# First MLP of a two-layer backbone: another order of the weight sums and of the squares, and other places for some pieces of the conditioning

## The chip, the cores and the metric

The kernel runs on one core of a Trainium2 chip. The metric is the time on the device, in microseconds, of one execution: the median of several runs. The engines are named as in the profile: PE multiplies matrices (PEld is its loading of weights), DVE, ACT and POOL do the elementwise work, SP issues most of the DMA transfers.

## What is computed

Two layers of width 1024 run over 512 latent and 256 context tokens, 768 rows in all. Each layer has a mixer (pooling in the first, attention in the second) and an MLP with 4096 hidden columns and a squared ReLU. Shift, scale and gate of every sub-layer come from a conditioning vector through the matrix `w_ada`. The reference, cut to what the change touches:

```python
def ada_mods(cond, w, b):
    m = (jax.nn.silu(cond) @ w + b)[..., None, :]
    return jnp.split(m, N_MOD, axis=-1)          # SH1 SC1 GT1 SH2 SC2 GT2

def modulate(h, shift, scale):
    return h * (1.0 + scale) + shift

def sq_relu_mlp(h, w_in, w_out):
    return jnp.square(jax.nn.relu(h @ w_in)) @ w_out
```

## The kernel before

**Precision.** Every operand of a large product is split into a high and a low part. One product of two operands is three matmuls: high by high, high by low, low by high. A split is a copy on ACT (the high part, `CAST` in the trace) and a subtraction on DVE (the low part).

**Phase one of the first MLP** (`mlp0`, the loop over g from 2 to 15) makes 256 hidden columns in each step, a *group*, for 768 tokens. It uses a seven-product scheme for 2 by 2 blocks, so each group is seven *chains* of 12 matmuls (`Seven.chain`), numbered 0 to 6 here, each 128x384. The weight operands of a group are the blocks B11, B21, B22 and the sums T1 = B12 − B11, T2 = B22 − T1, T3 = B22 − B12, T4 = B21 − T2, all split. `weights_sums(g + 1, raw)` makes those of the next group while the seven chains of this one run: the B pair and the pair T1, T2 go into `units`, and T3, T4 and B22 into `ra` (odd groups) or `rb` (even groups). Chain 1 uses T1, chain 2 T2, chain 3 B21, chain 4 T3, chain 5 B22 and chain 6 T4.

`Seven.run` issues the chains, copies each bank where the next chain needs it, and calls `behind(n)` between them. The lists in `behind` hold the steps of `weights_sums`, the sums over rows of a finished pair of groups (`left_sums`, four in each even group, written to DRAM by POOL's queue for phase two), and the conditioning dots. The two hidden rows `r0` and `r1` of a group go through a ReLU and a square on ACT into one of two `hiddens` tiles. `r0`, `r1` and the two tiles of differences come from a pool of three work tiles, in the order T1/T2, r1, T3/T4, r0.

**Phase two** (`Halves.run`) multiplies the hidden rows by the second matrix: 49 multiplies of 18 matmuls 128x512. In step j it starts the transfer for j + 5 (`load`), multiplies j, and prepares the operands for j + 3 (`prepare`: two copies on ACT, two or three subtractions on DVE). Multiplies 0 to 13 are the first pass, 14 to 27, 28 to 41 and 42 to 48 the others.

**The conditioning of the second layer** is made in *pieces* of 1 MB of `w_ada`, 256 columns each. A piece is loaded (`ask`) and then multiplied on DVE by a row of the conditioning vector and summed (`ada_dot`, a `CUSTOM_DVE` instruction over 128x1024 with a short read of the sum behind it): two such dots for a piece that only the latents need, four for one that the context needs too. 24 pieces go this way: 14 in phase one (52 dots), 10 in phase two (20 dots). The last gate, GT2 of layer 1, is instead summed in the output stage of attention by `ada_sum` (per piece eight multiply-adds 128x256, a transpose and a reduction on DVE) and finished by `ada_fin` with four small matmuls on PE in the second MLP. The gate and the other parts of layer 0 that are needed early use PE (`ada_mm`, `ada_rows`, `ada_sel`, `ada_mods`: matmuls 32x512 or 32x256, a transpose on DVE, four matmuls with `sel`, and a short finish).

**What sets the order.** In phases one and two the order of each engine's instructions is that of the program text (`pin(True)`). Elsewhere a planner places the steps by numbers given to `at` and `st.at`. The raw weights and pieces share a pool of three 1 MB tiles, `rawp`, in the order of their issue on SP's queue.

**The output stage of attention** (`output`) projects the heads (`psy`, bank by bank into `acc` on DVE), adds the result to the residual rows `xr` (L411), norms them (L637, or L635 on ACT) and transposes them on PE (`psx`) for the second MLP.

## Time and profile before

| what | us |
|---|---|
| median of 3 runs | 1181.74 (1181.52 to 1184.62) |
| the profiled execution's own time | 1181.55 |
| span of its trace | 1179.4 |
| phase one, first matmul of g = 2 to the first of phase two | 109.25 to 363.57 |
| phase two, to the first matmul behind it | 363.57 to 575.97 |
| output stage of attention, about | 793 to 843 |

The span is the time between the first and the last instruction that the trace shows; the profiled execution's own time holds 2.15 us more around it. The page of the profile gives the busy time of each engine and groups of instructions; the timeline lists instructions with their start, duration and, in brackets, the idle time before them and what ended it.

### The profile page before, as it was taken

How to read it: one execution, taken by the hardware profiler on the slowest of the kernel's cores; microseconds unless marked ns; L12 is line 12 of the kernel's file. 1: busy time of each engine (PE TensorE's matmuls, PEld its weight loads, DVE VectorE, ACT ScalarE, POOL GpSimd, SP SyncE). 2: the span in 40 equal slices, each digit the busy share in tenths (PEclk: the TensorE clock that was granted, in tenths of full speed). 3: DMA queues.
4: the chain of work that ended last, by engine and by line, in shares of the span. 5: the costliest groups of instructions: out<-in, count | busy, mean ns of one | idle time of the engine just before them, and what ended most of it. 6: DMA issues, size and time to landing. Idle time of an engine off the chain costs nothing.

```text
span 1179.4 us, 15819 instructions
## 1 busy us (share of the span) xinstructions
PE 1119.8 (95%) x6030; PEld 969.1 (82%) x6030; DVE 928.2 (79%) x1319; ACT 618.1 (52%) x1035; POOL 105.3 (9%) x176
## 2 busy tenths in 40 slices
PE   7999788888899999999999999999999999999997
PEld 6779788877888877788888889998988888888886
DVE  5788787788777978997778679968677789778886
ACT  6686354454446444343476357763577346435523
POOL 1230010110110000000032210001100000000001
PEclk9999999999999999999999999999999999999999
DMA  9975554554649999996612101105334233213203
GB/s 376 418 291 133 189 191 168 218 201 174 232 150 347 385 360 352 369 385 237 257 63 81 59 14 59 50 1 196 134 134 143 69 110 143 108 36 143 107 26 117
DMA packets 52506, 213.12 MB, mean 181 GB/s; under 512 B 7408, under 2 KB 10304, under 8 KB 37840
## 3 DMA queue, kind: packets, MB, share of 16 engines
q1 hardware_dynamic: 45824, 185.52, 43.1%
q0 software_dynamic: 6608, 26.61, 6.1%
q8 instruction: 47, 0.77, 0.3%
q14 instruction: 27, 0.22, 0.0%
HBM read 178.16 MB, written 33.96 MB: 180 GB/s over the span
## 4 chain that ended last, share of the span: by engine, by line
PE 72%; DVE 13%; ACT 6%; issue 4%; DMA 2%; POOL 2%; SPq 0%; ACTq 0%; DVEq 0%; POOLq 0%
PE psin L682 14%; PE pso L94 12%; PE pso L1275 11%; PE psin L94 9%; PE pso L950 5%; PE psq L1398 4%; PE psy L1682 3%; PE po L1658 3%; DVE work L94 3%; PE pss L1617 3%; DVE acc L94 2%; DVE waste L94 2%; PE pspt L1639 2%; DVE units L94 2%; DMA raw<-in_w_ada 1%
## 5 line engine op out<-in xcount | busy, mean ns | idle before, releaser
L94 PE MATMUL pso<-ra,sums 128*128 128x512 f32 x594 | 139.0, 394 | 4.1 <-DVE ra L94 2.2
L94 PEld LDWEIGHTS pso<-ra,sums 128*128 128x128 f32 x594 | 112.3, 190 | 29.8 <-DVE ra L94 4.3
L94 DVE CUSTOM_DVE_ANT_0 waste<-raw,crow 128x1024 f32<-128x1024 f32 (+1 forms) x72 | 88.0, 1222 | 11.6 <-DMA raw<-in_w_ada 10.4
L682 PE MATMUL psin<-ra,rb 128*128 128x512 f32 (+1 forms) x310 | 87.8, 360 | 0.0
L1275 PE MATMUL pso<-units,pairs 128*128 128x512 f32 x336 | 82.7, 389 | 0.0
L94 ACT CAST ra<-work 128x1024 fp32r<-128x1024 f32 x34 | 35.6, 1047 | 83.3 <-DVE work L94 81.6
L682 PE MATMUL psin<-ra 128*128 128x512 f32 (+1 forms) x256 | 76.5, 376 | 0.0
L1275 PEld LDWEIGHTS pso<-units,pairs 128*128 128x128 f32 x336 | 63.1, 188 | 13.1
L1279 DVE TENSOR_TENSOR acc<-acc,pso 128x512 f32<-128x512 f32 x72 | 48.7, 682 | 26.3 <-PE pso L1275 26.3
L94 PE MATMUL psin<-sums,units 128*128 128x384 f32 x336 | 63.2, 338 | 4.5 <-ACT psin L94 3.6
L94 PE MATMUL psin<-ra,units 128*128 128x384 f32 x340 | 65.8, 343 | 0.0
L94 PEld LDWEIGHTS psin<-sums,units 128*128 128x128 f32 x336 | 58.2, 188 | 7.6 <-ACT psin L94 6.1
L682 PEld LDWEIGHTS psin<-ra,rb 128*128 128x128 f32 x310 | 55.6, 189 | 8.7
L94 PEld LDWEIGHTS psin<-ra,units 128*128 128x128 f32 x340 | 62.3, 196 | 0.0
L94 ACT ACTIVATE work<-psin 128x384 f32<-128x384 f32 x28 | 13.8, 492 | 91.5 <-PE psin L94 60.5
L94 PE MATMUL pso<-ra,rb 128*128 128x512 f32 x252 | 59.3, 391 | 2.2 <-DVE ra L94 2.2
L242 POOL TENSOR_SCALAR ms<-ss 128x1 f32<-128x1 f32 x15 | 9.7, 645 | 567.7 <-ACT junk L229 547.6
L94 PEld LDWEIGHTS pso<-ra,rb 128*128 128x128 f32 x252 | 47.1, 188 | 13.3 <-DVE ra L94 3.2
L94 DVE TENSOR_TENSOR ra<-work,ra 128x1024 fp32r<-128x1024 f32 x34 | 41.7, 1226 | 19.1 <-ACT ra L94 19.1
L682 PE MATMUL psin<-rb,rb 128*128 128x512 f32 (+1 forms) x155 | 55.9, 362 | 0.6 <-DVE rb L1751 0.6
L682 PEld LDWEIGHTS psin<-ra 128*128 128x128 f32 x256 | 47.1, 188 | 8.7
L1398 PE MATMUL psq<-units,ra 128*128 128x512 f32 x216 | 52.4, 393 | 0.0
(328 smaller groups left out, 2688.3 us busy)
## 6 DMA issues: line engine op xcount, KB each, us to landing
raw<-in_w_ada SPq DMA_DIRECT2D x48, 1024.0 KB, 9.6
raw<-in_w_mlp_in SPq DMA_DIRECT2D x32, 1024.0 KB, 5.1
lefts<-acc POOLq DMA_DIRECT2D x48, 384.0 KB, 5.8
raw<-in_w_mlp_out SPq DMA_DIRECT2D x18, 1024.0 KB, 5.7
wide<-lefts SPq DMA_DIRECT2D x38, 384.0 KB, 6.9
wide<-in_w_mlp_out SPq DMA_DIRECT2D x21, 512.0 KB, 6.3
halfway<-work POOLq DMA_DIRECT2D x14, 512.0 KB, 7.3
raw<-in_w_mlp_out SPq DMA_DIRECT2D x14, 512.0 KB, 7.6
```

The lines of the kernel that those rows point to most:

```text
L94: return lambda *args, **kw: self.tc.keep_in_program_order(f(*args, **kw))
L242: gp.tensor_scalar(out=ms[:, 0:1], in0=ss[:, parts - 1:parts], scalar1=rest, scalar2=EPS, op0=ALU.add, op1=ALU.add)
L682: te.matmul(ps[:, bank, o:o + ln], w[:, k, fs], rhs, start=start, stop=(k == KT - 1 and n == 2), skip_group_check=len(ks) < KT or self.paired)
L950: te.matmul(pss[h][:, 0:cols[h][1]], a[:, f, ts_], w[:, f, cols[h][0]:sum(cols[h])], start=(n == 0 and not seeded[t]), stop=(n == len(seq) ...
L1275: te.matmul(ps, a, w, start=(m == 0), stop=(m == len(seq) - 1))
L1279: ve.tensor_tensor(out=M[n][:, t], in0=M[n][:, t], in1=ps, op=ALU.add)
L1398: te.matmul(ps, a[:, k, sl], w[:, k % 4, :], start=(k == 0 and n == 0), stop=(k == KT - 1 and n == 2))
L1617: te.matmul(ps[:, c2, 0:384], a[:, sl], b[:, kv, 384 * c2:384 * c2 + 384], start=(n == 0), stop=(n == 2))
L1639: te.transpose(ps[:, j, :], p[:, k * P:(k + 1) * P], ident)
L1658: te.matmul(po[:, 0:256], v, p, start=(n == 0), stop=(n == len(seq) - 1))
L1682: te.matmul(ps, a[:, k, sl], w[:, k % 4, o:o + width], start=(k == 0 and n == 0), stop=(k == KT - 1 and n == 2))
```

## The change

In words, by place:

- *Phase one, weights.* One subtraction 128x1024 makes T1 and T3 together; then the B pair is split, then T1/T3 (now in `units`), and later T2 and T4 are made (two subtractions 128x512) and split with B22 into `ra` or `rb`. There are three subtractions for the sums in place of four.
- *Phase one, rows.* `r0` is written by its ReLU straight into the hidden rows and squared there, so that a group uses three work tiles. The ReLU of `r1` and both squares of a group are issued in the next group, behind its chain 0. Three of the row sums stand behind chain 2 and the fourth behind chain 4. The dots stand at the end of a group, behind chains 5 and 6.
- *Pieces.* Phase one has 12 pieces (40 dots), in the order two of four dots, one of two; they go to groups 2 to 13. Phase two has 5 (10 dots), asked at j = 5, 11, 16, 21 and 25. Seven pieces (SH2 1 to 3 and the four of GT2 of layer 1) are loaded and multiplied by dots in the output stage, with the conditioning row in `gate`; `ada_sum` and `ada_fin` are gone. GT2 of layer 0 goes through PE in phase two, in two halves: two loads of 1 MB each at j = 2 and 15, eight matmuls three steps later, the transpose a step behind them, `sel` after the next, then the finish.

In the rows that follow, L94 (before) and L95 (after) are the helper that issues phases one and two in program order, and other numbers move by some lines between the two kernels.

**Phase one, ACT, from one odd group's end into the even group behind it** (`work<-work` is the ReLU of `r1`, `acc<-` are squares or, after, the ReLU of `r0`; `units` holds the weight splits). Before:

```order
L94 CAST rb<-raw 128x512
L94 ACTIVATE work<-psin 128x384
L94 ACTIVATE work<-work 128x768
L94 ACTIVATE acc<-work 128x768 x2
L94 COPY psin<-psin 128x384
L94 CAST units<-raw 128x1024
L94 COPY work<-psin 128x384
L94 CAST units<-work 128x1024
L94 COPY psin<-psin 128x384
L94 ACTIVATE work<-psin 128x384
L94 CAST ra<-work 128x2x4x128
L94 COPY work<-psin 128x384
```

The same place of the changed kernel:

```order
L95 CAST rb<-raw 128x512
L95 ACTIVATE acc<-psin 128x384
L95 CAST units<-raw 128x1024
L95 COPY psin<-psin 128x384
L95 CAST units<-work 128x1024
L95 ACTIVATE work<-work 128x768
L95 ACTIVATE acc<-work 128x768
L95 ACTIVATE acc<-acc 128x768
L95 COPY work<-psin 128x384
L95 COPY psin<-psin 128x384
L95 ACTIVATE acc<-psin 128x384
L95 CAST ra<-work 128x2x4x128
```

The two splits into `units` stand ahead of the ReLU of `r1` and of both squares, which stood ahead of them; and the first ReLU (`<-psin`) writes `acc`, the hidden rows, in place of a work tile.

**Phase one, DVE, an even group** (`ISA waste<-` with the short row behind it is a dot; `acc<-acc` are row sums; `work<-raw` and `work<-raw,work` make the T's). Before, from its last dot on:

```order
L94 ISA waste,mods_94<-raw,crow 128x1024
L94 ISA mods_94 128x1
L94 TENSOR_TENSOR work<-raw 128x512
L94 TENSOR_TENSOR work<-raw,work 128x512
L94 TENSOR_TENSOR ra<-work,ra 128x2x4x128
L94 TENSOR_TENSOR acc<-acc 128x768
L94 TENSOR_TENSOR work<-work 128x384
L94 TENSOR_TENSOR ra<-raw,ra 128x4x128
L94 TENSOR_TENSOR acc<-acc 128x768
L94 TENSOR_TENSOR work<-work,psin 128x384
L94 TENSOR_TENSOR acc<-acc 128x768 x2
```

After, from its first subtraction to the first dot:

```order
L95 TENSOR_TENSOR work<-raw 128x1024
L95 TENSOR_TENSOR units<-raw,units 128x1024
L95 TENSOR_TENSOR units<-work,units 128x1024
L95 TENSOR_TENSOR work<-raw,work 128x512 x2
L95 TENSOR_TENSOR acc<-acc 128x768 x3
L95 TENSOR_TENSOR ra<-work,ra 128x2x4x128
L95 TENSOR_TENSOR work<-work 128x384
L95 TENSOR_TENSOR ra<-raw,ra 128x4x128
L95 TENSOR_TENSOR acc<-acc 128x768
L95 TENSOR_TENSOR work<-work,psin 128x384
L95 ISA waste,mods_95<-raw,crow 128x1024
```

The dots have gone from the middle of the group to its end, three of the four row sums stand together ahead of the low part of T2/T4, and T1/T3 is one instruction.

**Phase two, PE** (`pso` are the multiplies, 18 matmuls each; `psada` the gate of layer 0). From the start of the phase in the changed kernel; before, there are no `psada` rows at this place:

```order
L95 MATMUL pso<-sums 128x512 x18
L95 MATMUL pso<-sums,rb 128x512 x18
L95 MATMUL pso<-ra,rb_103 128x512 x36
L95 MATMUL pso<-ra,sums 128x512 x36
L95 MATMUL psada<-raw,cond 32x512 x8
L95 MATMUL pso<-ra,sums 128x512 x36
L95 MATMUL psada<-work,sel 32x2x4 x4
L95 MATMUL pso<-ra,sums 128x512 x18
L95 MATMUL pso<-ra,rb_103 128x512 x36
L95 MATMUL pso<-ra,sums 128x512 x90
L95 MATMUL pso<-ra,rb_103 128x512 x36
L95 MATMUL pso<-ra,sums 128x512 x18
```

Eight matmuls 32x512 stand behind multiply 5, and four with `sel` behind multiply 7; the second half stands the same way behind multiplies 18 and 20. On DVE the transpose that `sel` needs stands behind the two dots of step 6:

```order
L95 TENSOR_TENSOR rb<-acc,rb 128x1536
L95 ISA waste,mods_95<-raw,crow 128x1024
L95 ISA mods_95 128x1
L95 ISA waste,mods_95<-raw,crow 128x1024
L95 ISA mods_95 128x1
L95 STREAM_TRANSPOSE work<-psada 128x512
L95 TENSOR_TENSOR rb_103<-wide,rb_103 128x768
L95 TENSOR_TENSOR ra<-wide,ra 128x1024
```

**Output stage, DVE** (`rb<-raw` are splits of weights, `rows` the work of `ada_sum`). Before, from the first residual to the second:

```order
L411 SCALAR_TENSOR_TENSOR xr<-acc,rs,xr 128x1024
L326 TENSOR_SCALAR rows<-raw,cond 128x256
L408 TENSOR_TENSOR acc<-psy,gate 128x512
L326 TENSOR_SCALAR rows<-raw,cond 128x256
L331 SCALAR_TENSOR_TENSOR rows<-raw,cond,rows 128x256 x4
L637 TENSOR_SCALAR acc<-xr,rs 128x1024
L331 SCALAR_TENSOR_TENSOR rows<-raw,cond,rows 128x256 x4
L1700 TENSOR_TENSOR rb<-raw,rb 128x1024
L331 SCALAR_TENSOR_TENSOR rows<-raw,cond,rows 128x256
L408 TENSOR_TENSOR acc<-psy,gate 128x512
L331 SCALAR_TENSOR_TENSOR rows<-raw,cond,rows 128x256 x5
L411 SCALAR_TENSOR_TENSOR xr<-acc,rs,xr 128x1024
```

The changed kernel, from the first residual to the second:

```order
L385 SCALAR_TENSOR_TENSOR xr<-acc,rs,xr 128x1024
L382 TENSOR_TENSOR acc<-psy,gate 128x512
L324 ISA raw,mods_95<-raw,gate 128x1024
L324 ISA mods_95 128x1
L324 ISA raw,mods_95<-raw,gate 128x1024
L324 ISA mods_95 128x1
L382 TENSOR_TENSOR acc<-psy,gate 128x512
L611 TENSOR_SCALAR acc<-xr,rs 128x1024
L1699 TENSOR_TENSOR rb<-raw,rb 128x1024
L332 TENSOR_TENSOR mods_95<-mods_95,vec 128x8
L385 SCALAR_TENSOR_TENSOR xr<-acc,rs,xr 128x1024
```

Of the seven pairs of dots one stands ahead of the stage's splits, one among them and the rest between the additions of the banks (`acc<-psy`), the last behind the first residual; `ada_sum` is gone.

The diff, cut to its core:

```diff
+LATER, ALONE = 5, 9
...
+    def ada_mm(i, m, j, w=2, zs=None, raws=None):
...
+            raw = (raws[z] if raws else raw_load(w_ada[i, m, j + z])).rearrange("p (k n) -> p k n", n=w * P)
...
-    def ada_sum(i, m, j, nc_, part):
-        raw = raw_load(w_ada[i, m, j]).rearrange("p (k n) -> p k n", n=256)
...
-        for k in range(1, KT):
-            for c, r in enumerate(rows):
-                ve.scalar_tensor_tensor(out=r, in0=raw[:, k, :], scalar=cond[:, k, c:c + 1], in1=r,
-                                        op0=ALU.mult, op1=ALU.add)
...
-        def difference():
-            tt, t1, t2 = low(0)
-            ve.tensor_tensor(out=t1, in0=b12, in1=b11, op=ALU.subtract)
-            ve.tensor_tensor(out=t2, in0=b22, in1=t1, op=ALU.subtract)
-
-        def difference2():
-            tu, t3, t4 = low(1)
-            ve.tensor_tensor(out=t3, in0=b22, in1=b12, op=ALU.subtract)
-            ve.tensor_tensor(out=t4, in0=b21, in1=k4(w[0][:, 512:1024]), op=ALU.subtract)
-
-        steps = [lambda: put(home[:, 0:2048], rv[:, 0], 1024), difference,
-                 lambda: put(home[:, 2048:4096], k4(w[0]), 1024), difference2,
-                 lambda: put3(0, 2, w[1].rearrange("p (m k n) -> p m k n", m=2, n=P)),
-                 lambda: put3(2, 1, b22.unsqueeze(1))]
+        words = lambda z: z.rearrange("p (m k n) -> p m k n", m=2, n=P)
+
+        def first_two():
+            w[0] = work_tile()
+            ve.tensor_tensor(out=words(w[0]), in0=rv[:, 1].rearrange("p (m k) n -> p m k n", m=2),
+                             in1=rv[:, :, 0:4], op=ALU.subtract)
+
+        def last_two():
+            w[1] = work_tile()
+            t2, t4 = (k4(w[1][:, 512 * m:512 * m + 512]) for m in range(2))
+            ve.tensor_tensor(out=t2, in0=b22, in1=k4(w[0][:, 0:512]), op=ALU.subtract)
+            ve.tensor_tensor(out=t4, in0=b21, in1=t2, op=ALU.subtract)
+
+        steps = [first_two, lambda: put(home[:, 0:2048], rv[:, 0], 1024),
+                 lambda: put(home[:, 2048:4096], k4(w[0]), 1024), last_two,
+                 lambda: put3(0, 2, words(w[1])), lambda: put3(2, 1, b22.unsqueeze(1))]
...
-            behind(0)
+            behind(1)
             self.chain(e, 1, True, True)
             r1 = work_tile()[:, 0:TOK]
             sc.copy(r1[:, 0:HN], e)
-            behind(1)
+            behind(2)
             self.chain(a, 2, False, False)
             sc.copy(c, a)
-            behind(2)
+            behind(3)
             self.chain(b, 3, False, True)
-            r0 = work_tile()[:, 0:TOK]
             sc.activation(r0[:, 0:HN], b, AF.Relu)
-            behind(3)
+            behind(4)
             self.chain(a, 4, False, False)
             sc.copy(r1[:, HN:TOK], a)
             ve.tensor_tensor(out=r1[:, HN:TOK], in0=r1[:, HN:TOK], in1=r1[:, 0:HN], op=ALU.add)
-            behind(4)
+            behind(5)
             self.chain(c, 5, False, True)
             ve.tensor_tensor(out=r1[:, 0:HN], in0=r1[:, 0:HN], in1=c, op=ALU.add)
-            behind(5)
+            behind(6)
             self.chain(a, 6, False, True)
             sc.activation(r0[:, HN:TOK], a, AF.Relu)
-            sc.activation(r1, r1, AF.Relu)
-            for f, r in enumerate((r0, r1)):
-                sc.activation(self.to[:, f, :], r, AF.Square)
-            behind(6)
+            behind(7)
+
+            def squares():
+                sc.activation(r1, r1, AF.Relu)
+                sc.activation(to1, r1, AF.Square)
+                sc.activation(r0, r0, AF.Square)
+
+            return squares
...
-            behind = [[] for _ in range(7)]
+            behind = [[] for _ in range(8)]
             if g < NG - 1:
                 steps, products = weights_sums(g + 1, raw)
                 for n, z in enumerate(steps):
-                    behind[(0, 0, 1, 2, 3, 4)[n]].append(z)
+                    behind[(0, 0, 1, 2, 4, 5)[n]].append(z)
+
+            def rows_done(squares=squares, g=g):
+                squares()
+                if g % 2 and g < 2 * PAIRS:
+                    left_keep(g // 2, 0, hiddens[0][:, :, 0:HN])
+                if g % 2 == 0 and 2 < g <= 2 * PAIRS:
+                    due[:] = left_sums(g // 2 - 1, *hiddens)
+
+            behind[1].append(rows_done)
             if g % 2 == 0:
-                for n, z in enumerate(due):
-                    behind[(3, 4, 5, 5)[n]].append(z)
+                behind[3].append(lambda: [due[n]() for n in range(3)])
+                behind[5].append(lambda: due[3]())
             if asked:
                 for n, z in enumerate(asked.pop(0)):
-                    behind[(1, 6)[n]].append(z)
+                    behind[6 + n].append(z)
             if g < NG - 2:
                 raw = raw_load(w_mlp_in[0, g + 2])
-            if g < NG - 1:
+            if g < NG - 1 and len(work) > LATER:
                 ask(*work.pop(0))
-            else:
+            if g == NG - 1:
                 chain.begin()
-                behind[4].append(lambda: chain.prepare(0))
-                behind[6].append(lambda: chain.prepare(1))
-            seven.run(lambda z: [f() for f in behind[z]])
-            if g < 2 * PAIRS:
-                if g % 2:
-                    due = left_sums(g // 2, *hiddens)
-                else:
-                    left_keep(g // 2, 0, hiddens[0][:, :, 0:HN])
+                behind[5].append(lambda: chain.prepare(0))
+                behind[7].append(lambda: chain.prepare(1))
+            squares = seven.run(lambda z: [f() for f in behind[z]])
             if g == 4:
                 head_gains()
             if g == 8:
                 ve.tensor_scalar(out=grow[:, 0, :], in0=grow[:, 0, :], scalar1=float(HD) ** -0.5, scalar2=None, op0=ALU.mult)
+        squares()
         chain.run()
...
-                if work and j % 2 and j > 2:
+                if work and j in (5, 11, 16, 21, 25):
                     ask(*work.pop(0))
+                for n, k in enumerate((2, 15)):
+                    what = (0, GT2, 2 * n)
+                    if j == k:
+                        wide_raws = [raw_load(w_ada[0, GT2, 2 * n + z]) for z in range(2)]
+                    elif j == k + 3:
+                        ada_mm(*what, 4, None, wide_raws)
+                    elif j == k + 4:
+                        ada_rows(*what)
+                    elif j == k + 5:
+                        ada_sel(*what)
+                    elif j == k + 6:
+                        ada_mods(*what)
...
-            if p == 1:
-                ada_fin(1, GT2, parts[1], 1)
...
-    work = [(i, m, j, 2) for i, m in ((0, GT2), (1, SC1), (1, SH1)) for j in range(4)]
-    work += [(1, m, j, 1) for m in (GT1, SC2, SH2) for j in range(4)]
+    alone = [(1, m, j, 1) for m in (GT1, SC2, SH2) for j in range(4)]
+    duals = [(1, m, j, 2) for m in (SC1, SH1) for j in range(4)]
+    work = [z for n in range(4) for z in (duals[2 * n], duals[2 * n + 1], alone[n])] + alone[4:ALONE]
+    late_work = alone[ALONE:] + [(1, GT2, j, 1) for j in range(4)]
+
+    def ask_late(i, m, j, nc_):
+        raw = raw_load(w_ada[i, m, j])
+        for b in range(2):
+            ada_dot(i, m, j, nc_, raw, [gate[:, 1, :]], raw[:, D * b:D * b + D], b)
...
+        at(38, lambda: sy.dma_start(gate[:, 1, :], silu[0].partition_broadcast(P)))
...
-        parts[1] = small.tile([P, 32], F32, tag="part", name="part", bufs=1)
-        for j in range(4):
-            at((7, 12, 17, 25)[j], ada_sum, 1, GT2, j, 1, parts[1][:, 8 * j:8 * j + 8])
+        for n, what in enumerate(late_work):
+            at((3, 6.5, 10, 13.5, 17, 21, 25)[n], ask_late, *what)
```

## The prediction

> **What bounds the kernel now.** I read the page first (busy time, then the chain that ended last), and then the timeline of single engines in the stages that the change touches.

> ```profile
> PE 1119.8 (95%) x6030; PEld 969.1 (82%) x6030; DVE 928.2 (79%) x1319; ACT 618.1 (52%) x1035; POOL 105.3 (9%) x176
> ...
> PE 72%; DVE 13%; ACT 6%; issue 4%; DMA 2%; POOL 2%; SPq 0%; ACTq 0%; DVEq 0%; POOLq 0%
> ```

> PE is the bound, but 28% of the chain that ended last runs over others. The timeline of PE in phase one says where: one odd group (203.59 to 222.93), the even one behind it, and the last three chains.

> ```profile
> 109.25 2.59 PE L94 MATMUL psin<-ra,units 128*128 128x384 f32 x14
> ...
> 203.59 2.24 PE L94 MATMUL psin<-ra,units 128*128 128x384 f32 x12
> ...
> 208.43 2.36 PE L94 MATMUL psin<-sums,units 128*128 128x384 f32 x12 [0.52 <-ACT psin L94]
> ...
> 213.60 0.45 PE L94 MATMUL psin<-sums,ra 128*128 128x384 f32 x1 [0.72 <-ACT psin L94]
> ...
> 220.01 3.12 PE L94 MATMUL psin<-ra 128*128 128x384 f32 x12 [1.98 <-ACT work L94]
> 222.93 3.10 PE L94 MATMUL psin<-ra,units 128*128 128x384 f32 x12
> ...
> 238.01 2.38 PE L94 MATMUL psin<-ra,rb 128*128 128x384 f32 x12 [1.57 <-ACT work L94]
> 240.22 2.24 PE L94 MATMUL psin<-ra,units 128*128 128x384 f32 x12
> ...
> 361.49 2.24 PE L94 MATMUL psin<-ra 128*128 128x384 f32 x12
> 363.57 4.28 PE L94 MATMUL pso<-sums 128*128 128x512 f32 x18
> ```

> A chain without a wait takes 363.57 − 361.49 = 2.08, so a group needs 7 × 2.08 = 14.56. The 14 groups take 363.57 − 109.25 = 254.3, or 18.2 each: **50 us above the floor of 203.8**. A pair takes 36.6 (203.59 to 240.22). Chain 6 waits for ACT in both groups (1.98, 1.57), chains 2 and 4 in the odd one. What ACT waits for stands in its rows and DVE's:

> ```profile
> 235.35 0.68 DVE L94 TENSOR_TENSOR work<-raw,work 128x512 f32<-128x512 f32 x1
> 236.15 0.49 ACT L94 ACTIVATE work<-psin 128x384 f32<-128x384 f32 x1 [4.61 <-DVE work L94]
> 236.54 1.04 ACT L94 CAST ra<-work 128x1024 fp32r<-128x1024 f32 x1
> 237.47 0.48 ACT L94 COPY work<-psin 128x384 f32<-128x384 f32 x1
> ```

> `r0`'s ReLU needs a work tile, and it stands idle 4.61 until DVE, with four dots in each group, has made T3 and T4. The copy that chain 6 waits for is two instructions behind it. So this stage is a DVE chain with PE hung on it.

> **Phase one after the change.** The work tile of `r0` is gone and with it this wait. I lay out DVE and ACT by these groups:

> ```profile
> L94 DVE CUSTOM_DVE_ANT_0 waste<-raw,crow 128x1024 f32<-128x1024 f32 x33 | 40.3, 1221 | 0.6
> L94 DVE TENSOR_TENSOR acc<-acc 128x768 f32<-128x768 f32 x19 | 17.7, 951 | 0.0
> L94 DVE TENSOR_TENSOR work<-raw 128x512 f32<-128x512 f32 x18 | 12.3, 685 | 0.0
> L94 DVE TENSOR_TENSOR units<-raw,units 128x1024 fp32r<-128x1024 f32 x9 | 11.0, 1223 | 11.6 <-ACT units L94 11.6
> ...
> L94 ACT CAST units<-work 128x1024 fp32r<-128x1024 f32 x9 | 9.4, 1048 | 17.9 <-DVE work L94 17.9
> L94 ACT ACTIVATE acc<-work 128x768 f32<-128x768 f32 x16 | 12.6, 836 | 0.3
> L94 ACT COPY work<-psin 128x384 f32<-128x384 f32 x18 | 8.6, 479 | 2.5 <-PE psin L94 2.5
> ```

> Back to back each runs about 0.09 below its mean, since starts overlap ends (236.54 to 237.47 is 0.93 for a cast of 1.04); a dot takes 1.26 with its read. Take the group's first matmul as 0.

> - *What is late next.* Chain 4 writes a bank that ACT must first have copied (after chain 2). Ahead of that copy ACT now has: the cast of T1/T3, the ReLU and two squares of the group before, and two copies. From the end of DVE's first subtraction that is 0.95 + 3 × 0.74 + 0.40 + 0.48 = 4.1. PE is ready at 4 × 2.08 = 8.3. If the subtraction ends at F, PE waits F + 4.1 − 8.3.
> - *After an odd group with four dots:* DVE's last sum ends at −1.4, dots 4 × 1.26 = 5.0, subtraction 1.2: F = 4.9, wait 0.7, group 15.4 with the restart.
> - *Inside an even group* three row sums (2.6) stand ahead, and `r0`'s ReLU, which overwrites what they read, follows at 11.1; then ReLU, cast and low part, the other small splits and the fourth sum end at 16.2, 0.8 past the group's end. With four dots F = 0.8 + 5.0 + 1.2 = 7.0: wait 2.9, odd group 17.6. With two dots 15.1. From a group that began without lag, four dots give 16.2.
> - *Sum.* Groups 4 to 15 by their dots: 15.4, 15.1, 15.4, 17.6, 14.6, 16.2, 15.4, 15.1, 15.4, 17.6, 14.6, 14.6 = 187.0. For groups 2 and 3, whose first operands come as late as before, 17.9 and 17.4. In all 222.3 against 254.3: **−32**. Laid out the same way, the kernel before gives 254.6 to 255.6, so the method is good to a microsecond or two there. Of the 32 the fewer dots (40 instead of 52) are about 6; the order has most of it.

> *The clock.* From 220.01 to 222.93, after a wait of 1.98, a chain took 2.92 and not the 2.21 of 238.01 to 240.22; the window over it and the next:

> ```profile
> 220.00:226.00 6.00, 5.99 (x25) 5.99 (x26) 4.75 (x8) 3.17 (x5) 0.00 (x0) 0.72 0.49 169
> ```

> Second number PE's busy time, last but two the granted clock: 0.72 with PE busy throughout. A clock of 0.72 over 6.0 costs about 1.6. Three other groups of phase one show the same, and all of it is hidden, since DVE sets the pace (this even group takes 17.3 all the same). After, PE sets it, and a drop counts. Waits of 2.9 stay in two groups and some near 1 to 2; I take one drop and a bit, **+2** (0 to +6).

> [...]

> **Phase two.**

> ```profile
> 398.86 1.22 DVE L94 CUSTOM_DVE_ANT_0 waste<-raw,crow 128x1024 bf16<-128x1024 f32 x1
> ...
> 441.93 0.50 PE L94 MATMUL pso<-ra,sums 128*128 128x512 f32 x1 [1.72 <-ACT ra L94]
> ...
> 506.61 20.56 PE L94 MATMUL pso<-ra,sums 128*128 128x512 f32 x90
> 527.01 8.32 PE L94 MATMUL pso<-ra,rb 128*128 128x512 f32 x36
> ...
> 575.97 1.55 PE L401 MATMUL psg<-diag,onesr 128*128 128x512 f32 x6
> ```

> ```profile
> 430.00:500.00 70.00, 63.91 (x264) 50.06 (x264) 59.48 (x72) 26.48 (x31) 3.13 (x6) 0.98 0.98 366
> ```

> Five multiplies take 527.01 − 506.61 = 20.40, so 49 take 199.9; the phase takes 575.97 − 363.57 = 212.4. Of the 12.5 over it, 70 − 63.91 = 6.1 are idle time of PE in 430 to 500, where the DMA engines are busy 0.98 and prepared operands come late (1.72 at 441.93). Added is the gate on PE, priced by its rows in the first stage:

> ```profile
> 40.13 1.07 PE L94 MATMUL psada<-raw,cond 128*32 128x512 f32 x8
> 41.12 0.98 PE L94 MATMUL pspool<-rb,ra 128*128 128x256 f32 x6
> ...
> 44.65 0.25 PE L94 MATMUL psada<-work,sel 128*32 128x8 f32 x8
> ```

> Eight records, which are four matmuls, take 0.99: sixteen are **4.0**; `sel` twice 0.25 each half, 0.5. `sel` adds a wait: it needs the transpose, which stands on DVE behind the dots of step 6, which need their load. Before, those dots began at 398.86; PE comes to `sel` behind eight multiplies, near 400. With one load more ahead of them I take 3 to 5 us of waiting there and 2 to 3 at the second half. Queued behind `sel` on PE is multiply 8; its operands and those of 9 and 10 are prepared meanwhile. Against this, 9 MB of pieces come in place of 10, and 10 dots in place of 20 stand on DVE ahead of `prepare`:

> ```profile
> L94 DVE CUSTOM_DVE_ANT_0 waste<-raw,crow 128x1024 f32<-128x1024 f32 (+1 forms) x72 | 88.0, 1222 | 11.6 <-DMA raw<-in_w_ada 10.4
> ```

> Ahead of the dots DVE waits 10.4 for their loads; the 12.5 bound what its end can return, and I take 9. 4.5 + 6.5 − 9 = 2, and while PE stands at `sel` the loads behind it go on, which the later part needs: **0** (−6 to +7).

> **Output stage.**

> ```profile
> 825.94 1.29 DVE L411 SCALAR_TENSOR_TENSOR xr<-acc,rs,xr 128x1024 f32<-128x1024 f32 x1 [0.85 <-POOL rs L244]
> ...
> 829.47 1.15 ACT L635 ACTIVATE acc<-xr,rs 128x1024 f32<-128x1024 f32 x1 [0.18 <-POOL rs L244]
> ...
> 830.73 0.38 PE L432 MATMUL psx<-ident,acc 128*128 128x128 f32 x2
> ```

> ```profile
> L331 DVE SCALAR_TENSOR_TENSOR rows<-raw,cond,rows 128x256 f32<-128x256 f32 x28 | 12.6, 480 | 0.5
> ```

> ```profile
> raw<-in_w_ada SPq DMA_DIRECT2D x4, 1024.0 KB, 4.8
> ```

> The second residual, its norm and the transpose on PE follow each other without slack. DVE's work stays: 14 dots × 1.26 = 17.6 for 12.6 and some 4.6 of short instructions. New is the load: seven pieces pass through three tiles that `w_in` uses too, and each load starts when the dots of an earlier tile end. A load lands 4.8 later; the instructions between two pieces cover 1 to 2 of it. For two of the pieces ahead of the second residual that leaves about 3 and 4, less 2 of idle time there: **+5** (0 if the loads start early enough, +8 if three pieces wait). `ada_fin` takes away four matmuls, −0.3.

> **Sum**, against the profiled execution: 1181.55 − 32 + 2 + 0 + 5 − 0.3 = 1156.2. The median of the runs is 0.2 above that execution, so the two are one. A measurement here can tell 0.3%, 3.5 us, from no change.

> **The rivals.**

> 1. *Better:* the clock holds (−2), and loads cover the output stage or phase two returns more (−3 to −9): 1145 to 1150. For it: the idle time of 430 to 500; against: each step must go well. 0.13.
> 2. *The new waits on PE and for the pieces are dearer:* +7 in phase two and +8 in the output stage: 1156 + 7 + 3 = 1166, to 1170 with the clock at +6. For it: zero slack in both places. 0.12.
> 3. *DVE stays the bound.* Its work for a pair is 14.7 for the splits and sums, 3.5 for the row sums and, at 40 dots in twelve groups, 6.7 × 1.26 = 8.4: 26.6, below the 29.1 of PE. If it also stands 1.3 ahead of each of six low parts, as now (11.6 over nine rows of `units`), a pair takes 34.4 in place of 36.6, phase one gains 13, and the time is 1175. For it: DVE is busy 79%. Against it: PE's copies and the new order put ACT's casts earlier than DVE needs them. 0.08.
> 4. *Slower:* the first ReLU writes straight into the rows that POOL's queue still reads for `lefts`.

> ```profile
> lefts<-acc POOLq DMA_DIRECT2D x48, 384.0 KB, 5.8
> ```

> The transfers are issued some 8 us into a group, and the ReLU that overwrites them comes at 8.3 in the next: about 15 of slack against a median of 5.8. Beyond 15 each microsecond of landing costs one per pair, six pairs; the 25 that the sum gains and 3.5 more, over six pairs, are 4.8 each, so from about 20 us it is slower by over 0.3%: at 20.5, 1189. Against it: the median. 0.04.
> 5. *No change:* another resource holds the pace of phase one, as the DMA engines do in 430 to 500: 1179 to 1183. Against it: the window of phase one has them at 0.49. 0.03.

> **How the numbers follow.** The forecast (1150 to 1165) has 0.60. Range 1145 to 1170: the forecast, the better case and the dearer waits hold 0.85, of which some 0.05 lies beyond the two ends; the rest is DVE, no change and slower. Faster by over 0.3%: 0.60 + 0.13 + 0.12 + 0.08 = 0.93; within 0.3% 0.03; slower 0.04.

> **What would show it.** In phase one: no wait of `ACT work` at chain 6; waits at chain 4 in groups 7 and 13 of near 3, phase one 220 to 226 long; a `PE` row of 12 matmuls near 3 where the clock drops. In phase two: a wait for DVE at `psada<-work,sel`, length 206 to 219. In the output stage: dots waiting for `raw<-in_w_ada`, the second residual 5 later against the start of the stage. The forecast is wrong if phase one keeps 18 us groups, or if the time gained is given back between 576 and 793, which the change does not touch.

## The result, and the profile after

The changed kernel takes 1170.39 us (median of 4 runs, 1169.33 to 1171.17) beside 1181.63 (1180.97 to 1184.62) for the kernel before: a ratio of 0.9899, 95% interval 0.988 to 0.9918. That is 11.2 us less where 25.3 were forecast, and just above the range. The median given for `pad_order` below leaves out one execution of 1584.63, far slower than its three others; with it, it is 1158.67, the value by which a later expectation goes (5.3). The spans of the two profiled executions, 1179.4 and 1168.9, differ by 10.5. The starts of the first matmuls of each stage in PE's timeline divide it:

| stretch (first matmul to first matmul) | before | after | change | predicted |
|---|---|---|---|---|
| up to phase one | 109.25 | 109.64 | +0.4 | 0 |
| phase one (`psin` of group 2 to `pso`) | 254.3 | 228.9 | −25.4 | −32 + 2 |
| phase two (`pso` to `psg`) | 212.4 | 219.6 | +7.2 | 0 |
| layer 0's end and attention (`psg` to `psy`) | 216.6 | 218.9 | +2.3 | 0 |
| output stage (`psy` to `psx`) | 38.2 | 38.7 | +0.5 | +5 |
| second MLP and the end (`psx` to the last instruction) | 348.7 | 353.2 | +4.5 | −0.3 |

The page of the changed kernel, busy times:

```profile
PE 1127.1 (96%) x6070; PEld 973.4 (83%) x6070; DVE 905.5 (77%) x1252; ACT 618.3 (53%) x1035; POOL 107.5 (9%) x176
```

PE's busy time has *risen* by 7.3 us, and the added matmuls of the gate are 4.1 of them. What else changed for PE, stretches of halved clock at other places and slower matmuls, follows.

**Phase one.** PE's timeline of the changed kernel: the start, group 7 (189.24 to 210.07) with its wait, a shorter wait in group 9, the wait of group 13, and the first row of phase two.

```profile
109.64 2.63 PE L95 MATMUL psin<-ra,units 128*128 128x384 f32 x14
...
189.24 2.27 PE L95 MATMUL psin<-ra,units 128*128 128x384 f32 x12
...
195.54 2.27 PE L95 MATMUL psin<-ra,units 128*128 128x384 f32 x12
200.98 0.69 PE L95 MATMUL psin<-sums,units 128*128 128x384 f32 x1 [3.17 <-ACT psin L95]
...
204.99 3.16 PE L95 MATMUL psin<-rb,ra 128*128 128x384 f32 x12
207.99 2.24 PE L95 MATMUL psin<-ra 128*128 128x384 f32 x12
210.07 2.27 PE L95 MATMUL psin<-ra,units 128*128 128x384 f32 x12
...
235.23 0.45 PE L95 MATMUL psin<-sums,units 128*128 128x384 f32 x1 [1.80 <-ACT psin L95]
...
299.96 0.69 PE L95 MATMUL psin<-sums,units 128*128 128x384 f32 x1 [2.95 <-ACT psin L95]
...
338.55 4.29 PE L95 MATMUL pso<-sums 128*128 128x512 f32 x18
```

The wait at chain 6 is gone but for some 0.3 in four of the even groups, and the long wait has moved to chain 4. DVE's subtraction in group 7 and ACT's timeline behind it show the chain of work that the prediction laid out, from the end of the subtraction to the copy:

```profile
195.53 1.22 DVE L95 TENSOR_TENSOR work<-raw 128x1024 f32<-128x1024 f32 x1
...
196.78 1.05 ACT L95 CAST units<-work 128x1024 fp32r<-128x1024 f32 x1 [4.77 <-DVE work L95]
197.74 0.84 ACT L95 ACTIVATE work<-work 128x768 f32<-128x768 f32 x1
...
200.45 0.48 ACT L95 COPY psin<-psin 128x384 f32<-128x384 f32 x1
```

From the end of the subtraction (196.75) to PE's next matmul (200.98) it is 4.2, where 4.1 was laid out. But the two chains behind the wait take 207.99 − 200.98 = 7.0 in place of 4.2. The windows of the changed kernel over the two long waits, and over the short one of group 9 (last but two is the granted clock):

```profile
199.00:209.00 10.00, 8.02 (x30) 8.02 (x31) 4.73 (x8) 4.27 (x8) 0.71 (x1) 0.66 0.26 75
296.00:309.00 13.00, 10.05 (x42) 9.73 (x41) 7.67 (x11) 6.22 (x10) 0.71 (x1) 0.74 0.39 146
...
233.00:240.00 7.00, 5.20 (x30) 4.88 (x29) 4.43 (x7) 4.53 (x8) 0.71 (x1) 1.00 0.28 108
```

At 0.66 over 10 us the clock was halved for 6.8 (from 200.20 to 206.90 the trace has it at 0.50, and so from 299.20 to 305.90); that cost 2.8, and as much at 299.96.

**Phase two.** PE's timeline at the two `sel`:

```profile
377.08 0.25 PE L95 MATMUL psada<-work,sel 128*32 128x8 f32 x8 [3.45 <-DVE work L95]
377.26 6.01 PE L95 MATMUL pso<-ra,sums 128*128 128x512 f32 x18
383.11 8.33 PE L95 MATMUL pso<-ra,rb 128*128 128x512 f32 x36
...
426.03 1.07 PE L95 MATMUL psada<-raw,cond 128*32 128x512 f32 x8 [0.96 <-DMA raw<-in_w_ada]
...
438.82 0.25 PE L95 MATMUL psada<-work,sel 128*32 128x8 f32 x8 [3.34 <-DVE work L95]
439.00 10.05 PE L95 MATMUL pso<-ra,sums 128*128 128x512 f32 x36
```

Both waits are there, 3.45 and 3.34, near the 3 to 5 and 2 to 3 forecast. DVE's dots ahead of the two transposes had waited 1.18 and 7.51 for their piece. Behind each wait PE is slow, with a granted clock of 0.50 from 377.70 to 381.00 and from 439.10 to 442.40: the 18 matmuls of 377.26 take 5.85 to the next row, in place of 4.08. In the kernel before, too, the clock was halved once in this phase (0.50 from 443.30 to 446.60), from 443.24 for 3.4 us, behind the wait of 1.72 at 441.93; so the change adds one such stretch to the phase, not two.

**Output stage.** PE at the first product, and DVE ahead of it:

```profile
777.04 3.01 PE L1681 MATMUL psy<-ra 128*128 128x512 f32 x12 [0.91 <-DVE ra L1659]
```

```profile
774.27 1.22 DVE L324 CUSTOM_DVE_ANT_0 raw<-raw,gate 128x1024 f32<-128x1024 f32 x1 [2.60 <-DMA gate<-silu]
```

The first pair of dots waits for the conditioning row and stands ahead of the last piece of attention on DVE: 0.9. No dot waits for `raw<-in_w_ada`.

**The second MLP** is not touched by the change and is 4.5 longer. The groups of PE by form, first the kernel before, then the changed one:

```profile
L1275 PE MATMUL pso<-units,pairs 128*128 128x512 f32 x336 | 82.7, 389 | 0.0
...
L682 PE MATMUL psin<-ra 128*128 128x512 f32 x224 | 70.6, 389 | 0.0
```

```profile
L1269 PE MATMUL pso<-units,pairs 128*128 128x512 f32 x336 | 84.4, 394 | 0.0
...
L656 PE MATMUL psin<-ra 128*128 128x512 f32 x224 | 70.7, 389 | 0.0
```

The same matmuls, none of them waiting, last 394 ns each where they read `units`, and 389 as before where they read `ra` alone. What differs is where `units` lies. With `ada_sum` a tile of 128 bytes, `part`, has gone from the pool `small`, and `rb` and `units`, allocated behind it, have moved down, while `ra`, `sums` and `pairs` have stayed. Byte addresses in a partition, as the build gives them, and their remainder by 256:

```
           before          after
rb         100256 (160)    100128 (32)
units      124832 (160)    124704 (32)
ra, sums, pairs   (160)           (160)
```

### The profile page after: what moved, and what is told of

Its sections match the earlier page's. It is cut to its first block, busy times and chain, and to the rows that moved or that the text cites. A ratio compares the mean times of both kernels' runs of the same rounds, so it can differ in the third digit from the quotient of the medians.

```text
span 1168.9 us, 15825 instructions
## 1 busy us (share of the span) xinstructions
PE 1127.1 (96%) x6070; PEld 973.4 (83%) x6070; DVE 905.5 (77%) x1252; ACT 618.3 (53%) x1035; POOL 107.5 (9%) x176
## 4 chain that ended last, share of the span: by engine, by line
PE 71%; DVE 11%; ACT 7%; DMA 6%; issue 3%; POOL 1%; SPq 0%; DVEq 0%; POOLq 0%; ACTq 0%
PE psin L656 15%; PE pso L1269 12%; PE pso L95 10%; PE psin L95 8%; PE psq L1397 7%; PE pso L926 5%; DVE waste L95 4%; PE psy L1681 3%; DMA wide<-lefts 3%; PE pss L1616 3%; DVE work L95 3%; PE po L1657 3%; DMA raw<-in_w_ada 2%; PE pspt L1638 2%; ACT acc L95 1%
## 5 line engine op out<-in xcount | busy, mean ns | idle before, releaser
L95 PE MATMUL pso<-ra,sums 128*128 128x512 f32 x594 | 140.5, 397 | 1.1 <-DVE acc L95 1.1
L95 PEld LDWEIGHTS pso<-ra,sums 128*128 128x128 f32 x594 | 113.5, 192 | 27.1 <-DVE acc L95 1.5
L95 PE MATMUL psin<-sums,units 128*128 128x384 f32 x308 | 67.6, 354 | 10.4 <-ACT psin L95 10.4
L95 DVE CUSTOM_DVE_ANT_0 waste<-raw,crow 128x1024 f32<-128x1024 f32 (+1 forms) x50 | 61.1, 1223 | 14.6 <-DMA raw<-in_w_ada 13.4
L95 PEld LDWEIGHTS psin<-sums,units 128*128 128x128 f32 x308 | 57.6, 197 | 13.6 <-ACT psin L95 13.6
L95 ACT CAST ra<-work 128x1024 fp32r<-128x1024 f32 x34 | 35.6, 1048 | 57.1 <-DVE work L95 49.1
L95 PE MATMUL psin<-ra,units 128*128 128x384 f32 x340 | 64.3, 338 | 0.0
L95 PEld LDWEIGHTS psin<-ra,units 128*128 128x128 f32 x340 | 60.1, 188 | 0.0
L95 PE MATMUL pso<-ra,rb 128*128 128x512 f32 x252 | 58.7, 390 | 1.2 <-DVE ra L95 0.8
L95 PEld LDWEIGHTS pso<-ra,rb 128*128 128x128 f32 x252 | 47.2, 188 | 11.7 <-DVE ra L95 1.1
L95 DVE TENSOR_TENSOR ra<-work,ra 128x1024 fp32r<-128x1024 f32 x34 | 41.7, 1225 | 17.0 <-ACT ra L95 17.0
L95 POOL DMA_DIRECT2D lefts<-acc x48 | 30.0, 626 | 198.3 <-ACT work L95 141.6
## 6 DMA issues: line engine op xcount, KB each, us to landing
raw<-in_w_ada SPq DMA_DIRECT2D x48, 1024.0 KB, 10.8
raw<-in_w_mlp_in SPq DMA_DIRECT2D x32, 1024.0 KB, 4.9
lefts<-acc POOLq DMA_DIRECT2D x48, 384.0 KB, 3.8
raw<-in_w_mlp_out SPq DMA_DIRECT2D x18, 1024.0 KB, 5.5
wide<-lefts SPq DMA_DIRECT2D x38, 384.0 KB, 7.6
```

Of the source, the lines that this page charges most:

```text
L95: return lambda *args, **kw: self.tc.keep_in_program_order(f(*args, **kw))
```

## The experiments

Theory A from here on: PE is slower where its moving operand and its weights lie at different addresses modulo some power of two; phase one waits for DVE and ACT in odd groups and then loses the clock; phase two waits at `sel`. Rivals are named in each expectation.

**The tile put back** (`pad`). An unused tile in the pool where `part` was:

```diff
+        small.tile([P, 32], F32, tag="part", name="part", bufs=1)
         for n, what in enumerate(late_work):
```

> The changed kernel with one unused tile of 128 bytes per partition put back where the tile part of ada_sum stood, so that rb and units lie again at the addresses that they had before, against ra, sums and pairs, which never moved. Theory A (addresses): 128x512 matmuls go from 231 to 227 ns each and 128x384 from 175 to 173; phase one 2 shorter, the stretch from 558 to 690 about 1, the second MLP 4 to 4.5, in all 7 to 8: 1162.5. Rival B (the slower matmuls come from other work beside them, which a tile that nobody reads cannot change): 1170, within 1.

The run took 1163.97 (ratio to before 0.9836, 0.9821 to 0.9852), 6.4 less than the changed kernel, with the second MLP at 348.64 (348.68 before) and this row:

```profile
L1269 PE MATMUL pso<-units,pairs 128*128 128x512 f32 x336 | 82.7, 389 | 0.0
```

Phase two is 1.0 shorter, the attention 0.7, the output stage 0.5 and the second MLP 4.5. Phase one is not shorter (229.3; 228.8 in `pad_sel` below, whose phase one is the same program): there PE waits for ACT anyway. In this execution the clock was halved four times for 3.4 us in phase one, in groups 2, 7, 9 and 13, in place of twice for 6.8 in the changed kernel and in `pad_sel`. The theory holds, the 2 for phase one does not.

**Half of it put back** (`pad16`), `[P, 16]` in place of `[P, 32]`, so that the two sides differ by 64 bytes.

> As the changed kernel, with 64 bytes put back instead of 128: rb and units lie 64 bytes from their old places. If the cost depends on the difference of the two operands' addresses modulo 128 or 256 alone being zero, matmuls of a moved operand take more than 227 here too, and the time is near 1170; if only a difference of 128 costs, it is near 1162.5; if 64 costs more than 128, over 1171. Rival B: 1170, with 231 at the same matmuls as in the changed kernel.

Its one run took 1171.23, of which the second MLP 352.6: 64 bytes cost about as much as 128.

**The kernel before with the shift alone** (`before_shift`).

```diff
-        parts[1] = small.tile([P, 32], F32, tag="part", name="part", bufs=1)
+        parts[1] = small.tile([P, 40], F32, tag="part", name="part", bufs=1)
```

> The kernel before, with nothing changed but the tile part 32 bytes larger, so that rb and units lie 32 bytes further on against ra, sums and pairs. Theory A (addresses): any difference modulo 256 costs, so the second MLP takes 4 to 4.5 more, the stretch from phase two to the attention about 1, phase two about 1, phase one nothing (it waits for ACT, not for PE); 6 to 7 in all: 1188 to 1189. If 32 bytes are too few to matter: 1182. Rival B (other work beside the matmuls): 1182.

The run took 1189.42 (ratio 1.0067, 1.0047 to 1.0086): 7.3 slower by 32 bytes that nobody uses. The second MLP takes 353.95, 5.3 more, and its row is the next one. Phase two, for which 1 was expected, is 0.4 shorter, and phase one 1.2 longer.

```profile
L1275 PE MATMUL pso<-units,pairs 128*128 128x512 f32 x336 | 84.7, 395 | 0.0
```

The matmuls of five runs, sorted by the two addresses: median distance in ns from the start of a 128x512 matmul to the next, by its moving operand's address and that of the next matmul's weights, modulo 256:

```
               offset of rb, units    equal            different
before                 160            227 (x2847)      230 (x13)
pad                    160            227 (x2851)      230 (x14)
after                   32            227 (x1829)      232 (x1036)
pad16                   96            227 (x1829)      233 (x1036)
before_shift           192            227 (x1829)      234 (x1032)
```

In the changed kernel 1036 matmuls × 5 ns = 5.2 of the 6.4. In the column "equal" stand those with both operands moved, too: in these runs it is not the address of one that counts, but the difference. The sort does not single out the next matmul's weights, which are mostly in the same tile as a matmul's own: 84 matmuls whose moving operand lies at another offset than their own weights, but at that of the next one's, take 231, 234 and 232 in the three lower runs, and 227 in `pad` and the kernel before. So in these runs a matmul's own weights count; of the next one's these traces do not tell (12 matmuls the other way round take 232, 226 and 235).

**Other places for the dots of phase one** (`pad_order`).

```diff
-    work = [z for n in range(4) for z in (duals[2 * n], duals[2 * n + 1], alone[n])] + alone[4:ALONE]
+    work = [duals[0]] + [z for n in range(4) for z in (duals[n + 1], alone[n])] + duals[5:8] + alone[4:ALONE]
```

> As the run with the tile put back, and the twelve pieces of phase one in another order, so that four dots stand in groups 2, 3, 5, 7, 9, 11, 12, 13 and two in the even groups 4, 6, 8 and 10. Theory A: the long wait at chain 4 belongs to four dots behind an even group's row sums, so those of groups 7 (3.17) and 9 (1.80) become 0.4 or less, that of group 13 stays near 3; with the first goes its half-clock stretch (2.8): 6 to 8 less than with the tile alone. Rival B: the wait follows the number of dots in two groups, wherever they stand: within 2.

The run took 1158.07 (ratio 0.9783, 0.976 to 0.9806), 5.9 less than with the tile alone, a little under the 6 to 8 expected; phase one takes 223.2 in place of 229.3. PE's waits at chain 4 in groups 7, 9 and 13:

```profile
199.60 0.44 PE L95 MATMUL psin<-sums,units 128*128 128x384 f32 x1 [0.32 <-ACT psin L95]
...
231.12 0.44 PE L95 MATMUL psin<-sums,units 128*128 128x384 f32 x1 [0.48 <-ACT psin L95]
...
295.82 0.45 PE L95 MATMUL psin<-sums,units 128*128 128x384 f32 x1 [2.87 <-ACT psin L95]
```

The waits of 3.17 and 1.80 went with the dots, and the one of group 13, which kept its four, stayed: four dots behind an even group's row sums make it. After the 2.87 at 295.82 the clock stayed whole this time, and that was luck: of the 6.1 in phase one, some 1.5 came from it. Groups 7 and 9 give 4.5 and 3.2, waits and halved clock together, and groups 8 and 14, behind odd groups that now have four dots, take 1.7 and 1.4 back.

**Phase one alone** (`order_only`): the kernel before with the new `weights_sums`, `Seven.run` and loop, and every piece where it was; the loop differs from the change in one line:

```diff
-            if g < NG - 1 and len(work) > LATER:
+            if g < NG - 1:
                 ask(*work.pop(0))
```

> The kernel before with the change's phase one alone (weight sums, squares and row sums in the new order), and the pieces of conditioning where they were: 14 pieces in phase one, the first twelve of four dots each. Addresses as before. Theory A (a wait near 3 at chain 4 of each odd group behind four dots in an even one, and a half-clock stretch of 2.8 behind it): odd groups 18 to 21, even ones 15.5 to 16, phase one 240 to 247, the time 1167 to 1175. Rival (as the prediction had it, the order has most of the gain, without the clock): phase one 230 to 233, the time 1158 to 1161.

The run took 1169.61 (ratio 0.9892, 0.9857 to 0.9928); phase one takes 240.6. Five odd groups have the long wait. The first three of them, the first and the third with a halved clock behind the wait:

```profile
169.28 0.67 PE L94 MATMUL psin<-sums,units 128*128 128x384 f32 x1 [2.86 <-ACT psin L94]
...
204.57 0.45 PE L94 MATMUL psin<-sums,units 128*128 128x384 f32 x1 [2.87 <-ACT psin L94]
...
238.20 0.69 PE L94 MATMUL psin<-sums,units 128*128 128x384 f32 x1 [3.00 <-ACT psin L94]
```

So of the 25 in phase one the order has 13.7 and the fewer dots, added to it, 11.3 (240.6 to 229.3, at the same addresses), with the clock in both. The group without a drop takes 17.7, as the prediction's layout had it (17.6); the other four take 1.5 to 3.0 more, 8.9 together. Without them phase one would be near 231.7, an estimate from these lengths, and that is the 230 to 233 of the rival: the order does what the layout says, and the clock takes back a good part of it.

**`sel` later** (`pad_sel`).

```diff
-                    elif j == k + 5:
+                    elif j == k + 7:
                         ada_sel(*what)
-                    elif j == k + 6:
+                    elif j == k + 8:
                         ada_mods(*what)
```

> As the run with the tile put back, and the four sel matmuls of the layer 0 gate stand two steps of phase two later (behind multiplies 9 and 22 instead of 7 and 20), their finish too. Theory A: PE's two waits there (3.45 and 3.34) go, and with them the two half-clock windows behind them (about 1.8 each): phase two 219.6 becomes 209 to 211, the time 9 to 10 less than with the tile alone. Rival B: the transfers bound this phase, and the waits come back at multiplies between 430 and 500: 0 to 4 less.

The run took 1160.04 (ratio 0.9804, 0.9787 to 0.9822), 3.9 less than with the tile alone, which is the rival's size. Both waits at `sel` and both stretches of halved clock are gone (10 us), but phase two is only 3.5 shorter: PE now waits at multiplies from 453 on. Two rows of DVE show for what:

```profile
425.03 1.23 DVE L95 CUSTOM_DVE_ANT_0 waste<-raw,crow 128x1024 bf16<-128x1024 f32 x1 [7.74 <-DMA raw<-in_w_ada]
...
448.22 1.23 DVE L95 CUSTOM_DVE_ANT_0 waste<-raw,crow 128x1024 bf16<-128x1024 f32 x1 [5.32 <-DMA raw<-in_w_ada]
```

Whether the transfers of the multiplies or these dots bound PE is what the next two runs were for.

**All three** (`three`), and **all three with the pieces of phase two later** (`three_late`):

```diff
-                if work and j in (5, 11, 16, 21, 25):
+                if work and j in (8, 22, 27, 31, 35):
```

> The changed kernel with the tile put back, the pieces of phase one in the other order, and sel two steps later, together. If the three are independent (6.4, 5.3 and 3.9 less): 1154 to 1155. If the transfers bound phase two from an earlier start as well, less of it adds up: 1156 to 1158.

> As the run with all three, and the five pieces of phase two asked for at steps 8, 22, 27, 31 and 35 instead of 5, 11, 16, 21 and 25, away from the loads of the gate. Theory A (dots that wait for their load on DVE hold up the operands that PE waits for): the waits of 7.7 and 5.3 ahead of dots shrink, PE's waits between 440 and 480 too, and the time is 2 to 4 less than with all three. Rival B (the transfers of the multiplies themselves bound that stretch): within 1.

The two runs took 1152.77 (ratio 0.9756, 0.9738 to 0.9774) and **1147.12** (0.9707, 0.9688 to 0.9726), both faster than either kernel of this study. The first is 2 below the sum of the three parts (1154.8); in its phase one (221.7) the clock was not halved at all, which no expectation counted on. The second is 5.7 less, where 2 to 4 were expected. Its phase two takes 206.7 in place of 216.2, and DVE's waits ahead of dots, 9.24 and 4.98 in the first run, are 0.72 and 0.23. Against that stand 1.6 more in phase one, with a halved clock in group 13, and 1.5 more in the attention, whose cause stays open. The window that held 63.91 of PE's busy time in the kernel before reads as follows, first in `three` and then in `three_late`:

```profile
430.00:500.00 70.00, 63.94 (x277) 51.00 (x276) 59.32 (x73) 28.80 (x33) 1.06 (x2) 0.98 0.99 368
...
430.00:500.00 70.00, 69.39 (x312) 56.84 (x312) 63.69 (x80) 26.45 (x31) 0.53 (x1) 1.00 1.02 388
```

In the second run the DMA engines are busier than in any other (1.02, 388 GB/s), and PE hardly waits. So the transfers did not bound this stretch: dots that stood on DVE waiting for their piece held up the operands behind them. Of the two parts of the move, away from the gate's loads and later in the phase, these runs do not tell which did more.

## Why the prediction was wrong

- *Phase one, mechanism and layout: right.* Waits of 0.7, 2.9 and 2.9 were laid out for the groups behind four dots; 0.2 to 0.5, 3.17 and 2.95 were measured, and 4.2 from the subtraction to chain 4. Groups 7 and 13 were put at 17.6, and where the clock stayed whole such a group took 17.7 (`order_only`, `pad_order`).
- *The clock: mis-sized.* I took "one drop and a bit, +2". Two drops of 6.8 us came, one in each of the two groups with a long wait, 2.8 each: 5.6. Group 7 takes 210.07 − 189.24 = 20.8. The drops of the kernel before, 3.4 us long, had given the size. The rest of phase one was 1 above the layout, partly by luck: groups 2 and 3 were 2.5 below it, the others 3.5 above. What the drops cost is in part chance as well: phase one had none in `three`, and two of 6.8 or four of 3.4 in `pad_sel` and `pad`, with the same program for this phase. Nor does the length of a wait alone tell: behind 2.95 and 3.17 there was a drop here, behind the 2.87 in `pad_order` none. The last section says how the waits lay in these traces where a drop came.
- *The share of the order: wrong,* without changing the sum. "Of the 32 the fewer dots are about 6; the order has most of it": 13.7 and 11.3. With four dots everywhere five odd groups have the long wait and four of them the drop, 8.9 us that the layout leaves out; so it is the step on the clock again that failed.
- *Phase two: the sum lacked a term.* The gate's matmuls (4.1 against 4.0), the waits at `sel` (6.8 against 6.5) and what the fewer pieces return were near; the last, 8.8 against 9, is what is left over (4.1 + 0.5 + 6.8 + 3.6 + 1.0 − 7.2), measured by no run of its own, and 1.8 of it is the drop that the kernel before had in this phase. Not in it were the two drops of the clock behind these waits (1.8 each) and 1.0 for the addresses; and the step "while PE stands at `sel` the loads behind it go on", by which I took +2 down to 0, moved it the wrong way. The +7 of the range's end came out. Reading 430 to 500 as a stretch that busy DMA engines bound was wrong as well, as `three_late` shows for the changed kernel. For the kernel before it is argued only: of the 10.4 that DVE waits on the quoted row, 7.3 lie in this stretch, in four pieces, each 5 to 6 us ahead of a wait of PE.
- *Output stage: wrong, by 4.5.* "Each load starts when the dots of an earlier tile end", with 3 and 4 us of waiting: no dot waited for its piece. The one wait was for the conditioning row, 0.9, ahead of the stage.
- *The sum: its tacit step failed.* Code that the change does not touch was taken to keep its time. Taking a tile away moved others, and 6.4 of the 14 us between forecast and result went there. The sentence that time may be "given back between 576 and 793" looked at too small a place: 4.5 of the 6.4 went behind 815.

So 25.3 forecast became 11.2: 6.4 for the addresses (1.0 of it in phase two), 3.6 more than taken for the clock in phase one, 6.2 in phase two beside the addresses, 2.9 in small pieces, and 5.0 the other way in the output stage (4.5 net, as 0.5 of the addresses' share fell there).

## What to carry to other kernels

When a change adds or removes a tile, compare the addresses of all tiles that matmuls read, before and after: here a moving operand and weights at equal offsets modulo 256 ran at 227 ns, others at 230 to 234, and an unused tile repaired it (6.4 us less in `pad`). In a stage that PE bounds, count a stretch of halved clock behind each wait near 3 us (most of those here had one, at 1.5 to 3.0 us each in `order_only`), or spread the work (none came behind a full-clock window of 3.41 us with 1.73 or less of idle time); and before a difference of 2 us between two runs is explained, compare where their clock was halved. And when an engine works ahead for another, give it the instruction that needs a load only where the load has long landed: here the move of five pieces took phase two from 216.2 us to 206.7 (`three`, `three_late`).
